# Pinning the projections that run beside a sliding-window attention, and moving its output bank through ScalarE

## The chip, the cores and the metric

The kernel runs on one core of a Trainium2 chip. The core has a matrix engine (TensorE, PE in the profile, with its weight loads on a row of their own, PEld), three engines for elementwise work (VectorE is DVE, ScalarE is ACT, GpSimd is POOL), a sync engine (SP) that here issues nearly all DMAs, an SBUF of 128 partitions and a PSUM of eight banks. The metric is the device time of one execution in microseconds; a comparison takes the median of several runs.

## The reference, cut to what matters

Two sequences (1024 and 512 tokens, width 1024) pass through two layers with shared weights. The change touches layer 0 only:

```python
u = rmsnorm(x, norm_g[0]) @ w_in0
glu, a_gate, q, k, v, b_gate = split_cols(u, EVEN_SPLITS)
a_val, a_glu = jnp.split(glu, 2, axis=-1)
a = layernorm(depthwise_conv(a_val * sigmoid(a_glu), conv_w, conv_b), ln_g, ln_b)
a = silu(a) * silu(a_gate)
o = windowed_gqa(rope(q), rope(k), v, sink) * silu(b_gate)     # +-128 tokens, 8 heads, 2 key heads
x = x + concatenate([a, o]) @ w_out0
```

Layer 1 (differential attention beside a two-way state-space scan) starts from the norm of this x and is not touched.

## The kernel before, in words

Tokens are cut into three chunks of 512: chunks 0 and 1 are the long sequence (the prompt), chunk 2 is the short one (the sample). Every projection works on tiles of 128 output channels by 512 tokens. All numbers are fp32, split into a rounded high part and a remainder, so one tile is 8 slices of the inner dimension by 3 products, that is 24 matmuls of 128x512 (`proj`, lines 294 to 296). The weights of a tile come in two halves: a DMA (L281), a cast on ScalarE (L282) and a subtraction on GpSimd (L283).

The stages around the change, in program order:

- Phase A1: the gated inputs of the convolution, k, v and q (with rotary), and meanwhile the depthwise convolution on VectorE (`conv_units`). Then `conv_ln` (L490): its first matmul (L494) takes the mean over channels from a sum that VectorE completes at L486. Then `ag(0)` and `ag(1)`: gate tiles, each with three chunks; `gate2` (L384) evacuates a tile with two ScalarE activations (L386, L387) into two buffers of the tag `e2`, one VectorE multiply (L388) and a DMA to DRAM. In A1 the tag has four shared buffers and two more (`e2x`); the weights have three shared and two more per kind (`wrx`, `whx`, `wlx`). Five PSUM banks serve the projections.
- Phase A2: the sliding attention. `swa_units(1)` (sample) gives a start and 8 units, `swa_units(0)` (prompt) a start and 16; a unit is one block of 128 queries with one key head. In a unit, `scores` issues eight matmuls (L568, L569) for four heads, VectorE adds the band and takes the maximum (L572), ScalarE exponentiates (L574) and GpSimd scales (L582); `values` of the unit before transposes the probabilities (L597), splits them (L215, L216) and accumulates two products per block of keys (L600, L601) in one PSUM bank `oacc` (tag `ms`, one bank). ScalarE copies one half of the partitions out (L602) and VectorE adds the other half from PSUM (L603). `spread` (L1027) hands groups of other units out between these units: gate tiles `ag`, `bg`, the loads of the concatenated input of an output projection (`so[g][1]`, `cat_units`, L622) and its eight output tiles (`so[g][2]`, `tile_` in `out_units`, L640).
- Phase B1a: the output tiles of chunk 0 and 1, the norms (`out_norm`), and the first projections of layer 1.

What sets the order on each engine: the program is not run in the order in which it is written. A scheduler at build time simulates the time line with its own instruction costs, and issues on each engine whatever its simulation finds ready, earlier code first. The order that comes out is fixed: on the chip each engine runs its list in order, and an instruction that waits holds up all behind it. `tc.issue_after(x)` adds a rule to that scheduler: the instructions in the block that run on the engine of x come behind x in its list. It adds no wait on the chip.

Buffers of a phase are placed in SBUF in the order of the dictionary in `PHASES` (L39), each phase over the ones before it; a buffer of a new phase can be filled when the old buffers under it are done with. With the sizes in the code (2 KB a partition for `e2`, `wr`, `wh`, `wl`, 4 KB for `cs`, `raw`, `q6` and `k4`, 6 KB for `y6`), `raw` of A2 lies over `e2x`, `wrx` and `whx` of A1, and `q6`, the last entry of A2, over the `y6` buffers that hold the convolution's result until it is written to `cat0d` (L509).

## Time and profile before

| | us |
|---|---|
| median of 3 runs (lowest, highest) | 1651.07 (1649.37, 1654.11) |
| the profiled execution, its own time | 1646.57 |
| its span, first to last instruction | 1644.8 |
| PE busy in the span | 1541.7 |
| VectorE busy | 1092.4 |
| ScalarE busy | 747.4 |
| GpSimd busy | 670.8 |
| mean granted TensorE clock | 0.987 |

Stretches are given in us from the start of the span. Busy time of PE counts a matmul from its start to a modelled end, so PE can be called busy while matmuls come slower than they could. A row of a time line gives start, duration, engine, line and operation, and in brackets how long the engine was idle before it and what ended that. The layer that is changed takes the first 700 us or so; the stretch from 299 to 660 holds all that the change touches.

### The profile page before, as it was taken

The page shows a single profiled execution, that of the slowest core. Times are in us where ns is not written, and L with a number is a line of the kernel's source. Part 1 is how long each engine was busy: PE and PEld are TensorE (multiplying, and loading weights), DVE is VectorE, ACT ScalarE, POOL GpSimd, SP SyncE. Part 2 cuts the span into 40 slices and gives each one's busy share as a digit, 9 for nine tenths or more (in the row PEclk, how much of TensorE's full clock was granted, in tenths as well). Part 3 has the DMA queues.
Part 4 walks back from the last instruction along what each step waited for, and adds up shares of the span by engine and source line. Part 5 has one row for each costly group of instructions (what it writes and reads, how often), then busy time and mean ns, then how long its engine had stood idle before and what let it go on. Part 6 is the DMA issues. An engine that isn't in the chain of part 4 may idle for free.

```text
span 1644.8 us, 22557 instructions
## 1 busy us (share of the span) xinstructions
PE 1541.7 (94%) x7772; PEld 1280.1 (78%) x7772; DVE 1092.4 (66%) x1568; ACT 747.4 (45%) x1461; POOL 670.8 (41%) x555
## 2 busy tenths in 40 slices
PE   4999899699989899999999999999989999999897
PEld 3888787478857777778788888878878888888787
DVE  6699999866688857565542005786537678678663
ACT  6312111266777754345442112222227777668532
POOL 4333543226766647432211006654435535341530
PEclk9999999899999999999999999999999999999999
DMA  9221123244556558613333217754454445342561
GB/s 371 70 68 42 45 84 92 94 159 143 162 172 192 167 165 264 203 58 91 112 126 116 77 45 218 212 173 152 133 172 139 142 152 167 116 133 73 182 232 67
DMA packets 159108, 229.43 MB, mean 139 GB/s; under 512 B 18279, under 2 KB 70567, under 8 KB 158994
## 3 DMA queue, kind: packets, MB, share of 16 engines
q1 hardware_dynamic: 157074, 227.40, 43.8%
q8 instruction: 61, 1.00, 0.3%
q0 software_dynamic: 1920, 0.59, 0.2%
q14 instruction: 53, 0.43, 0.1%
HBM read 153.15 MB, written 64.55 MB: 132 GB/s over the span
## 4 chain that ended last, share of the span: by engine, by line
PE 34%; DMA 5%; DVE 4%; issue 3%; ACT 2%; POOL 2%; SPq 1%; POOLq 0%; DVEq 0%; ACTq 0%
PE pj L294 4%; PE pj L295 4%; PE pj L296 4%; PE ms L994 3%; PE pjx L759 2%; PE pjx L760 2%; PE pjx L761 2%; PE s L978 2%; PE s L979 2%; PE pjx L296 2%; PE pjx L295 2%; PE pjx L294 2%; PE tr L406 1%; PE trx L406 1%; DMA ct<-g2d 1%
## 5 line engine op out<-in xcount | busy, mean ns | idle before, releaser
L283 POOL TENSOR_TENSOR wl<-wr,wh 128x512 fp32r<-128x512 f32 (+1 forms) x147 | 210.1, 1433 | 277.7 <-ACT wh L282 265.6
L295 PE MATMUL pjx<-x,wh 128*128 128x512 f32 (+1 forms) x576 | 227.6, 395 | 5.6 <-DVE x L216 5.6
L294 PE MATMUL pjx<-x,wh 128*128 128x512 f32 (+1 forms) x576 | 228.3, 397 | 3.0 <-DVE e L395 1.0
L296 PE MATMUL pjx<-x,wl 128*128 128x512 f32 (+1 forms) x576 | 227.7, 396 | 3.3 <-POOL wl L283 3.3
L294 PE MATMUL pj<-x,wh 128*128 128x512 f32 x536 | 215.8, 403 | 12.5 <-ACT e L387 4.4
L295 PE MATMUL pj<-x,wh 128*128 128x512 f32 x536 | 211.8, 395 | 4.5 <-DVE x L216 4.5
L296 PE MATMUL pj<-x,wl 128*128 128x512 f32 x536 | 213.1, 398 | 0.0
L282 ACT ACTIVATE wh<-wr 128x512 fp32r<-128x512 f32 (+1 forms) x147 | 91.5, 623 | 130.5 <-PE pjx L295 49.4
L295 PEld LDWEIGHTS pjx<-x,wh 128*128 128x128 f32 (+1 forms) x576 | 107.4, 186 | 30.8 <-DVE x L216 6.8
L294 PEld LDWEIGHTS pj<-x,wh 128*128 128x128 f32 x536 | 101.8, 190 | 37.1 <-ACT e L387 6.4
L294 PEld LDWEIGHTS pjx<-x,wh 128*128 128x128 f32 (+1 forms) x576 | 107.3, 186 | 29.3 <-ACT x L215 1.8
L296 PEld LDWEIGHTS pjx<-x,wl 128*128 128x128 f32 (+1 forms) x576 | 107.1, 186 | 28.0 <-POOL wl L283 4.1
L295 PEld LDWEIGHTS pj<-x,wh 128*128 128x128 f32 x536 | 101.7, 190 | 25.9 <-DVE x L216 6.0
L296 PEld LDWEIGHTS pj<-x,wl 128*128 128x128 f32 x536 | 101.7, 190 | 21.5 <-issue 0.5
L980 DVE TENSOR_REDUCE nmx<-s 128x1 f32<-128x1024 f32 (+1 forms) x96 | 97.9, 1040 | 23.5 <-PE s L979 23.0
L982 ACT ACTIVATE pr<-s,nmx 128x1024 f32<-128x1024 f32 (+1 forms) x96 | 93.4, 975 | 32.7 <-DVE nmx L980 29.1
L191 POOL TENSOR_TENSOR r<-v,mhalf 128x4 f32<-128x4 f32 (+2 forms) x37 | 33.4, 901 | 128.8 <-DVE v L187 76.5
L994 PEld LDWEIGHTS ms<-v,pT 128*128 128x128 f32 x640 | 78.5, 191 | 6.8 <-ACT m L996 2.0
L994 PE MATMUL ms<-v,pT 128*128 128x128 f32 x640 | 81.3, 276 | 2.2 <-ACT m L996 1.2
L532 POOL TENSOR_TENSOR raw<-raw,q 128x1024 fp32r<-128x1024 f32 x24 | 59.1, 2462 | 49.3 <-ACT q L530 38.7
L836 POOL TENSOR_TENSOR xd<-x,ed 128x512 f32<-128x512 f32 x20 | 23.2, 1161 | 125.5 <-DMA x<-xbd 120.6
L283 POOL TENSOR_TENSOR wlx<-wrx,whx 128x512 fp32r<-128x512 f32 x20 | 51.4, 2578 | 55.4 <-ACT whx L282 55.4
(415 smaller groups left out, 3786.9 us busy)
## 6 DMA issues: line engine op xcount, KB each, us to landing
wr<-in_wo SPq DMA_DIRECT2D x84, 256.0 KB, 4.2
wr<-in_w SPq DMA_DIRECT2D x71, 256.0 KB, 3.6
x<-xbd SPq DMA_DIRECT2D x22, 384.0 KB, 4.4
ct<-x1d SPq DMA_DIRECT2D x29, 256.0 KB, 4.3
raw<-q0d SPq DMA_DIRECT2D x48, 128.0 KB, 3.1
ct<-cat0d SPq DMA_DIRECT2D x24, 256.0 KB, 4.7
x1d<-e SPq DMA_DIRECT2D x24, 256.0 KB, 3.9
raw<-q1d SPq DMA_DIRECT2D x48, 128.0 KB, 2.8
```

The source lines that it names most:

```text
L191: G.tensor_tensor(out=r[:, 0:n], in0=v[:, 0:n], in1=mhalf[:, 0:n], op=ALU.pow)
L282: S.activation(out=wh, in_=raw, func=AF.Copy)
L283: G.tensor_tensor(out=wl, in0=raw, in1=wh.bitcast(F32), op=ALU.subtract)
L294: T_.matmul(acc, wh[:, kk, :], xh[:, k, :], start=(k == ks[0]), stop=False)
L295: T_.matmul(acc, wh[:, kk, :], xl[:, k, :], start=False, stop=False)
L296: T_.matmul(acc, wl[:, kk, :], xh[:, k, :], start=False, stop=(k == ks[-1]))
L406: T_.transpose(pt[:, t, :], src[:, t * P:(t + 1) * P], ident)
L532: G.tensor_tensor(out=lo, in0=raw, in1=q.bitcast(F32), op=ALU.subtract)
L759: T_.matmul(acc, xh[:, k, ts], hi[k], start=(k == 0), stop=False)
L980: V.tensor_reduce(out=nmx[:, t:t + 1], in_=o, axis=AX.XY, op=ALU.max, negate=True)
L982: S.activation(out=pr, in_=o, func=AF.Exp, bias=nmx[:, t:t + 1], accum_out=den[:, t:t + 1])
L994: T_.matmul(oacc, pT[:, i, :], vtok[:, kt, :], start=(kt == 0), stop=(kt == NB - 1))
```

## The change

The tail of A1 is written as `ag(0)`, `ag(1)`, `ag(2)`, then `conv_ln` with its mean matmuls behind the last matmul of `ag(2)`, then `ag(3)`. In A2 every handed-out unit's PE instructions go behind the first score matmul of the newest attention unit written so far (`ph["pin"]`), and the groups get other places: the chunk 2 gate tiles of `bg(2)` and `bg(3)` and then `bg(0)` and `bg(1)` over places 0 to 9, the sample's concatenated input over 9 to 14, the rest of `bg` over 9 to 13, the sample's eight output tiles over 13 to 23 with the statistics of its norm (`norm_r`) as a ninth unit, chunk 0's input over 18 to 22 and two of its output tiles over 23 to 25; the other six follow the attention. Before, `ag(2)`, `ag(3)` and eight `bg` tiles stood over 0 to 7, and the sample's output tiles over 21 to 26. `values` copies the whole bank `oacc` into a new buffer `both` by ScalarE and adds its two halves from there. In A2 the buffer list is reordered: `q6` follows `raw`, the sample's keys get two buffers of their own (`k2`), `k4` goes from 3 to 2, `pr` (probabilities) from 10 to 9.

```diff
--- before.py
+++ after.py
@@ -38,7 +38,7 @@
 
 PHASES = {
     "A1": (dict(e2x=2, wrx=2, whx=2, wlx=2, cs=2, a=2, xs=1, fir=3, y6=5), dict(pjx=4, msx=1)),
-    "A2": (dict(raw=3, v2=1, k4=3, v4=1, ct=3, ss=1, m2=1, sq=1, pT=5, pr=10, q6=2), dict(pjx=1, s1=3, trx=1)),
+    "A2": (dict(raw=3, q6=2, k2=2, v2=1, m2=1, pr=9, pT=5, k4=2, v4=1, ct=3, ss=1, sq=1, both=1), dict(pjx=1, s1=3, trx=1)),
     "B1a": (dict(ct=10, ss=1, sq=1, dt=3, m2=3, a=3, y6=2), dict(pjx=4, msx=1)),
     "B1z": (dict(zr=2, zw=8, vw=8), dict(pjx=5)),
     "B1b": (dict(e2x=1, wrx=1, whx=1, wlx=1, rk=2, lk=4, cs=2, p4=4, x3=2, bc=2, xd=2, y=2, t=1, nx=4, pb=1, yc=2, zt=1), dict(sg=1, msx=2, trx=1)),
@@ -293,7 +293,7 @@
             with nullcontext() if after is None or k < k0 else tc.issue_after(after.ins):
                 T_.matmul(acc, wh[:, kk, :], xh[:, k, :], start=(k == ks[0]), stop=False)
                 T_.matmul(acc, wh[:, kk, :], xl[:, k, :], start=False, stop=False)
-                T_.matmul(acc, wl[:, kk, :], xh[:, k, :], start=False, stop=(k == ks[-1]))
+                ph["proj"] = T_.matmul(acc, wl[:, kk, :], xh[:, k, :], start=False, stop=(k == ks[-1]))
         return acc
 
     phase("A1")
@@ -487,11 +487,12 @@
 
         return [begin] + [lambda i=i: taps(i, i + 3) for i in range(1, 16, 3)] + [end]
 
-    def conv_ln():
+    def conv_ln(pin):
         sm = cvs["s"]
         for g in GO:
             mu = pm("ms")
-            T_.matmul(mu, mean_w, sm[:, g, :], start=True, stop=True)
+            with tc.issue_after(pin.ins):
+                T_.matmul(mu, mean_w, sm[:, g, :], start=True, stop=True)
             for j in range(4):
                 y = cv[j][:, g, :]
                 V.tensor_tensor(out=y, in0=y, in1=mu, op=ALU.subtract)
@@ -515,7 +516,7 @@
             raw = sb("raw", (P, T))
             for a in range(2):
                 dma(out=raw[64 * a:64 * a + 64], in_=src[64 * t:64 * t + 64, t0:t0 + T])
-            kt = sb("k4", (P, T), F32R)
+            kt = sb("k2" if T == CH and "k2" in ph["sb"] else "k4", (P, T), F32R)
             S.activation(out=kt, in_=raw, func=AF.Copy)
             G.tensor_tensor(out=kt[lr], in0=raw[lr], in1=kt[lr].bitcast(F32), op=ALU.subtract)
             kk.append(kt)
@@ -565,8 +566,10 @@
             prs = st_[b, g] = []
             for j in range(4):
                 o = pm("s1")[:, 0:nk * P]
-                T_.matmul(o, qh[:, g, j, :], kk[g][:, k0 * P:k1 * P], start=True, stop=False)
+                first = T_.matmul(o, qh[:, g, j, :], kk[g][:, k0 * P:k1 * P], start=True, stop=False)
                 T_.matmul(o, ql[:, g, j, :], kk[g][:, k0 * P:k1 * P], start=False, stop=True)
+                if j == 0:
+                    ph["pin"] = first
                 mx = nmx[:, j:j + 1]
                 pr = sb("pr", (P, 384))[:, 0:nk * P]
                 V.tensor_tensor_reduce(out=pr, in0=o, in1=band[:, (0 if k0 < b else P):(3 * P if k1 > b + 1 else 2 * P)], scale=-1.0,
@@ -599,8 +602,9 @@
                 split_into(pt, ph_, pl_, V)
                 T_.matmul(oacc, vtok[:, k0 + kb, g, :], ph_, start=(kb == 0), stop=False)
                 T_.matmul(oacc, vtok[:, k0 + kb, g, :], pl_, start=False, stop=(kb == nk - 1))
-            S.activation(out=ot[hr], in_=oacc[hr], func=AF.Copy)
-            V.tensor_tensor(out=ot[hr], in0=ot[hr], in1=oacc[64 - 64 * g:128 - 64 * g], op=ALU.add)
+            both = sb("both", QUAD)
+            S.activation(out=both, in_=oacc, func=AF.Copy)
+            V.tensor_tensor(out=ot[hr], in0=both[hr], in1=both[64 - 64 * g:128 - 64 * g], op=ALU.add)
             if g:
                 dma(out=catd[0][:, 4:8, t0 + b * P:t0 + (b + 1) * P], in_=ot)
 
@@ -656,8 +660,13 @@
 
         return st_, load(st_), [lambda j=j: tile_(j) for j in range(KT)]
 
+    def norm_r(st_):
+        st_["r"] = rstd_of(tok_sum([st_["ss"]]), 4, 1.0 / DM)
+
     def out_norm(st_, spill, g, gcol, last):
-        bc = tok_bcast(rstd_of(tok_sum([st_["ss"]]), 4, 1.0 / DM), 4, False)
+        if "r" not in st_:
+            norm_r(st_)
+        bc = tok_bcast(st_["r"], 4, False)
         if not last:
             xh, xl = x16(), x16()
         for k in range(KT):
@@ -1024,15 +1033,15 @@
         for u in f[j:]:
             u()
 
-    def spread(a, groups):
+    def spread(a, groups, pin=False):
         at = [[] for _ in range(len(a) + 1)]
         for f, p0, p1 in groups:
             for i, u in enumerate(f):
                 at[min(len(a), p0 + i * (p1 - p0) // len(f))].append(u)
         for i, u in enumerate(a):
-            run(at[i])
+            run(at[i], pin)
             u()
-        run(at[-1])
+        run(at[-1], pin)
 
     def tile_units(i, w, fn, order=(2, 0, 1)):
         st_ = {}
@@ -1060,9 +1069,10 @@
     def bg(j, order=N3):
         return tile_units(14 + j, w0, lambda acc, g: gate2(acc, gd[1][:, j, tok(g)]), order)
 
-    def run(us):
+    def run(us, pin=False):
         for u in us:
-            u()
+            with tc.issue_after(ph["pin"].ins) if pin and "pin" in ph else nullcontext():
+                u()
 
     gl = [glu_units(j) for j in range(4)]
     cu = [conv_units(j, gl[j][0]) for j in range(4)]
@@ -1073,23 +1083,27 @@
     merge(gl[2][1] + q[1], cu[1])
     merge(gl[3][1] + q[2], cu[2])
     merge(q[3] + q[4] + q[5], cu[3])
-    conv_ln()
-    run(ag(0) + ag(1))
+    run(ag(0) + ag(1) + ag(2))
+    conv_ln(ph["proj"])
+    run(ag(3))
 
     phase("A2")
     res0 = lambda g, j: xin(g)[:, j, :]
     so = [out_units(wo0, lambda st_, g=g: cat_units(st_, catd[0], {k: gd[k // 4] for k in range(8)}, g), res0, x1d, g, 4) for g in range(3)]
     uS, uP = swa_units(1), swa_units(0)
     spread(uS + uP, [
-        (ag(2) + ag(3) + bg(0) + bg(1) + bg(2, (2,)) + bg(3, (2,)), 0, 7),
-        (so[2][1], 11, 19),
-        (bg(2, (0, 1)) + bg(3, (0, 1)), 9, 17),
-        (so[0][1], 19, 19),
-        (so[2][2], 21, 26)])
+        (bg(2, (2,)) + bg(3, (2,)) + bg(0) + bg(1), 0, 9),
+        (so[2][1], 9, 14),
+        (bg(2, (0, 1)) + bg(3, (0, 1)), 9, 13),
+        (so[2][2] + [lambda: norm_r(so[2][0])], 13, 23),
+        (so[0][1], 18, 22),
+        (so[0][2][:2], 23, 25)], True)
+    run(so[0][2][2:4])
     out_norm(so[2][0], x1d, 2, PC_G1, False)
+    run(so[0][2][4:])
+    norm_r(so[0][0])
 
     phase("B1a")
-    run(so[0][2])
     run(so[1][1])
     out_norm(so[0][0], x1d, 0, PC_G1, False)
     run(so[1][2])
```

## Rows read from the trace of the kernel before

**Rows 1.** Busy time of each engine in eight stretches (columns: stretch, its length, PE, PEld, DVE, ACT, POOL with the number of instructions, granted TensorE clock, DMA share, GB/s).

```profile
299.00:324.00 25.00, 11.93 (x42) 8.72 (x41) 23.95 (x28) 5.09 (x9) 1.58 (x1) 0.73 0.23 79
324.00:378.00 54.00, 52.95 (x252) 43.30 (x252) 30.89 (x41) 31.74 (x51) 17.85 (x12) 1.00 0.55 180
378.00:461.00 83.00, 82.91 (x428) 69.85 (x427) 54.74 (x127) 60.40 (x147) 59.15 (x64) 1.00 0.49 149
461.00:500.00 39.00, 30.45 (x142) 21.36 (x140) 33.12 (x82) 29.05 (x78) 22.75 (x30) 0.96 0.53 155
500.00:555.00 55.00, 53.88 (x275) 45.36 (x274) 42.36 (x87) 39.09 (x91) 39.40 (x43) 1.00 0.61 187
555.00:589.00 34.00, 25.85 (x133) 19.11 (x131) 30.18 (x78) 25.95 (x69) 18.29 (x28) 0.95 0.57 181
589.00:610.00 21.00, 21.00 (x101) 17.30 (x100) 9.38 (x26) 9.42 (x20) 9.72 (x11) 1.00 0.45 133
610.00:660.00 50.00, 46.14 (x210) 37.56 (x209) 34.05 (x42) 21.94 (x39) 32.50 (x23) 0.97 0.80 252
```

**Rows 2.** The same stretches for L294 alone, the first of the three matmuls of a projection's slice (columns: stretch, length, PE, PEld with counts, clock, DMA share, GB/s); eight of them are one tile.

```profile
299.00:324.00 25.00, 5.44 (x13) 2.72 (x13) 0.73 0.23 79
324.00:378.00 54.00, 26.16 (x67) 12.43 (x67) 1.00 0.55 180
378.00:461.00 83.00, 32.17 (x82) 15.24 (x81) 1.00 0.49 149
461.00:500.00 39.00, 2.56 (x7) 1.24 (x8) 0.96 0.53 155
500.00:555.00 55.00, 19.73 (x49) 9.06 (x49) 1.00 0.61 187
555.00:589.00 34.00, 0.00 (x0) 0.01 (x1) 0.95 0.57 181
589.00:610.00 21.00, 10.47 (x26) 4.88 (x26) 1.00 0.45 133
```

**Rows 3.** The same for L568 alone, the first matmul of a head's scores; four of them are one attention unit.

```profile
378.00:461.00 83.00, 11.05 (x37) 6.76 (x37) 1.00 0.49 149
461.00:500.00 39.00, 8.07 (x21) 3.96 (x21) 0.96 0.53 155
500.00:555.00 55.00, 6.64 (x19) 3.58 (x19) 1.00 0.61 187
555.00:589.00 34.00, 7.38 (x19) 3.85 (x19) 0.95 0.57 181
```

**Rows 4.** Time line of PE from 304.9 to 324 us, cut.

```profile
304.57 0.39 PE L295 MATMUL pjx<-x,wh 128*128 128x512 f32 x1
304.80 0.39 PE L296 MATMUL pjx<-x,wl 128*128 128x512 f32 x1
...
305.93 0.39 PE L295 MATMUL pj<-x,wh 128*128 128x512 f32 x1
319.39 2.07 PE L494 MATMUL msx<-y,mean_w 128*128 128x512 f32 x2 [13.07 <-DVE y L486]
...
322.12 0.63 PE L295 MATMUL pj<-x,wh 128*128 128x512 f32 x1
322.54 0.63 PE L296 MATMUL pj<-x,wl 128*128 128x512 f32 x1
```

**Rows 5.** Time line of VectorE from 312 to 324 us: the last step of the sum that L494 reads.

```profile
317.58 1.76 DVE L486 TENSOR_TENSOR y<-y,y 128x1536 f32<-128x1536 f32 x1
```

**Rows 6.** Time line of ScalarE from 307 to 382 us, cut to the casts of the first keys and queries and the table load before the first exponential.

```profile
325.44 0.63 ACT L519 ACTIVATE k<-raw 128x512 fp32r<-128x512 f32 x1 [13.31 <-DMA raw<-k0d]
...
372.36 2.01 ACT L530 ACTIVATE q<-raw 128x1024 fp32r<-128x1024 f32 x2 [2.67 <-DMA cat0d<-y]
...
381.25 1.28 ACT L574 ACT_TABLE_LOAD   x1
```

**Rows 7.** Time line of SP's DMA issues from 319 to 367 us, cut.

```profile
319.96 0.32 SPq L389 DMA_DIRECT2D g0d<-e2x  x1
322.01 2.41 SPq L517 DMA_DIRECT2D raw<-k0d  x4
...
327.53 8.48 SPq L553 DMA_DIRECT2D raw<-q0d  x12
...
362.64 3.06 SPq L509 DMA_DIRECT2D cat0d<-y  x3
```

**Rows 8.** Time line of GpSimd from 320 to 382 us, cut: the subtractions of the first keys and of the first two queries.

```profile
326.20 2.66 POOL L520 TENSOR_TENSOR k<-raw,k 64x512 fp32r<-64x512 f32 x2 [15.60 <-ACT k L519]
...
373.50 5.22 POOL L532 TENSOR_TENSOR raw<-raw,q 128x1024 fp32r<-128x1024 f32 x2 [7.98 <-ACT q L530]
```

**Rows 9.** Time line of PE from 377.5 to 381 us: the first score matmuls.

```profile
378.09 0.52 PE L568 MATMUL s<-k,q 128*128 128x256 f32 x3
```

**Rows 10.** Two VectorE additions by line, over the sliding attention (columns: duration in ns as least, median and most; first and last start; form). The first has one input in PSUM, the second two in SBUF.

```profile
L603 DVE TENSOR_TENSOR m<-m,ms x24: 682/687/691, 403.0 to 610.0; 64x512 f32<-64x512 f32 x24
L655 DVE TENSOR_TENSOR ss<-ss,sq x9: 686/811/2885, 506.7 to 610.9; 128x512 f32<-128x512 f32 x9
```

**Rows 11.** Who waited for whom from 290 to 660 us (total us, times, longest), PE and VectorE, cut.

```profile
PE pjx L296 <- POOL wl L283: 3.3, 2, 2.8
...
PE ms L600 <- DVE m L603: 2.6, 3, 1.2
...
DVE pr L572 <- POOL pr L582: 2.3, 2, 1.2
DVE pr L572 <- PE trx L597: 2.0, 3, 0.8
```

## The prediction, made before the changed kernel was run

> **What bounds the kernel now.** PE is busy for 94% of the span, so only time in which it stands still or is slowed can be won. I cut the stretch that the change touches into eight and read engine times, then the count of projection matmuls (a tile is eight of L294) and of score matmuls (a unit is four of L568) [rows 1 to 3]. Three stretches stand out.
>
> First, 299 to 324: PE is busy for 11.9 of 25 us while VectorE is busy for 23.9 [rows 1]. The time line shows why. At 305.9 PE has begun the first tile of `ag(2)`, five matmuls in, and the next in its list is the mean matmul L494, which waits 13.07 us for L486, the end of the convolution on VectorE [rows 4, 5]. The projections behind it need nothing from it. The granted clock of the stretch is 0.73, and after the idle time matmuls start 0.42 us apart where they started 0.23 apart before [rows 4]: half of 2.4 GHz, until about 324.
>
> Second, the attention. In 378 to 461 and 500 to 555 PE is busy throughout (136.8 of 138 us). These hold 82 + 49 of L294, 16.4 tiles, and 37 + 19 of L568, 14 units. A tile takes 24 x 0.227 = 5.45 us [rows 4], so the tiles take 89 us and a unit (136.8 - 89) / 14 = 3.4 us of PE [rows 1 to 3]. In 461 to 500 and 555 to 589 there are only 7 of L294 and 40 of L568: 5 + 34 = 39 us of PE work in 73 us. So 34 us are lost where the units have no projections beside them; there VectorE is at 85% and 89% and paces them at 7.3 us a unit. In the two full stretches it is at 66% and 77%. The work is there, in the wrong place.
>
> Third, the first score comes only at 378.1 [rows 9]. The keys were cast at 325 and the query loads issued from 327.5, but the query cast waited until 372.4 for a write to `cat0d` [rows 6, 7]: `q6` lies over the convolution's result. By then ten tiles had been used up (80 of L294 from 299 to 378 [rows 2]) that the units lack later.
>
> **The change, part by part, against the profiled execution (1646.6).**
>
> *Front.* The matmuls of `ag(2)` no longer wait behind L494, and three tiles end at about 305.9 + 2.8 x 5.45 = 321, when the sum (319.3) is ready. The 13 us wait and the slow clock behind it (six and more matmuls with 0.2 us each and the slow L494 itself, some 2 to 3 us) go. What is late next is the first score. `q6` now lies over `wlx` and `cs`, free once the last `ag` tile has run, and `raw` still over `e2x`, `wrx`, `whx`, which `ag(3)` now uses. From 305.9 PE has 2.8 + 3 tiles of `ag`, so `ag(3)` ends near 338. Then the chain follows: key loads (2.4 us of issue), cast, subtraction 2.7, query loads (a third of 8.5), cast 1.0, subtraction 2.6 [rows 6 to 8], with some 3 us of landing each, about 18 us: the first score can come at 356 to 361. PE has for that time the two `bg` tiles that no pin holds and the small matmuls of `conv_ln` (about 8 us): 299 + 9.1 x 5.45 + 8 = 357. I take 361, for a few us of gap: 17 us won, between 4 (the evacuation of `ag(2)` stalls on `e2` buffers while VectorE still works off the convolution) and 21.
>
> The moved tiles take their queues with them: each of `ag(2)` and `ag(3)` issues two weight loads on SP (0.3 to 0.4 us each), two casts on ScalarE and two subtractions on GpSimd, now ahead of the key loads. At 305.9 the weights of `ag(2)` were there, and those of `ag(3)` have 15 us, so nothing for that. `conv_ln` is put off by some 2 us on PE; VectorE and ScalarE are its only waiters, and its result in `cat0d` is first read at place 9, tens of us later: nothing.
>
> *Loop.* The units must hold 12 `bg` tiles less 2, 8 + 2 output tiles: 20 tiles, where 20.5 ran before [rows 2]. PE needs 20 x 5.45 + 24 x 3.4 = 191 us of the 232 now spent. VectorE's 169.8 us (five stretches of rows 1) become some 178 with the dearer additions below; at the 0.87 it reaches where it sets the pace, 205 us. That is the floor. The ceiling is 228, the old length less half a tile: gates and concatenated loads crowd places 9 to 13 and 18 to 22, where VectorE has more than a unit's time to do. The pins keep a tile from being used before the unit ahead has begun, so the starved stretches should go, the crowded ones not. I take 216, the middle: 16 us won.
>
> *What is owed.* Fewer tiles are done by the end of the attention: 10 + 20.5 before, 9.1 + 20 after, 1.4 x 5.45 = 7.5 us to be paid there.
>
> *The copied bank.* ScalarE's copy costs the same: 128 or 64 partitions by 512 columns. `oacc` is released after the copy instead of after L603; PE waited 2.6 us in all for that [rows 11]. The addition takes two SBUF inputs. L603 never took over 0.69 us; L655, with two SBUF inputs, took 0.69 to 2.9, median 0.81 [rows 10], and GpSimd is busy for some 149 of these 232 us [rows 1]. So 24 additions cost 24 x 0.12 = 3 to 24 x 0.5 = 12 us of VectorE; I took 8 in the loop. The Trainium skill, SBUF — State Buffer, section SBUF: two separate sides, speaks against this edit: VectorE with two SBUF inputs and GpSimd exclude one another for a whole instruction. The spread of L655 beside the fixed L603 agrees; by the rule alone I would take the upper bound, 12 us instead of 8, and the loop's floor would be 209.
>
> *Smaller.* `pr` 10 to 9: VectorE waited 4.3 us for such buffers [rows 11]; one fewer may double that, 0 to 4 us, I take 1. Separate key buffers: no wait for them is seen, nothing. Exponentials may now fall between the SiLUs of `conv_ln`; each turn costs a table load of 1.28 us [rows 6] on ScalarE, which is busy 59% of the time then; 0 to 5, I take 0.5. The waits on weights at 630 to 640 (3.3 us [rows 11]) stay. `norm_r` early: its one short chain now lies beside units, nothing.
>
> Sum: -17 - 16 + 7.5 + 1.5 = -24, so 1622.6 profiled. The median lies 4.5 us above the profiled execution: 1627.
>
> **The rivals.**
>
> *Better.* Front 21 and loop 205: -21 - 27 + 7.5 = -40, 1611. For it: PE full for 138 us wherever projections stand beside units. Against: VectorE would have to hold 87% throughout.
>
> *VectorE paces the loop anyway.* The loop stays at 228: -17 - 4 + 9 = -12, 1639. For it: 85 and 89% in the starved stretches, and added work; against: 66 and 77% in the full ones.
>
> *The pinned mean changes little.* `ag(2)` is stuck behind the evacuation, VectorE being busy at 95% until 324 [rows 1]: front 4, loop 16: 1646.6 - 4 - 16 + 9 = 1636, 1640 by the median. Against: there are five banks, and PE had begun the first tile of `ag(2)` when it stopped.
>
> *Slower: whole tiles in the chain.* A pin fixes only the earliest place. If the scheduler, whose costs are not the chip's, places a tile's 24 matmuls in one piece between the first score and the rest of that unit, the unit's chain of score, maximum, exponential, transposes and products waits 5.45 us more: 7.3 + 5.45 = 12.7 us a unit, against 9 in the forecast, so each tile so placed costs 3.7 us. With 16 of 20 it costs 59: 1646.6 - 24 + 59 = 1682, 1686; with 10 it costs 37, 1664. It decides from 24 / 3.7 = 7 tiles on. Against: before, the tiles in the full stretches are cut into pieces between scores (the first score itself stands between two projection matmuls).
>
> *It does not do what it says.* The planner in its own time line had no starved stretch, and the tiles keep their places: what the front runs ahead is missing between the units later, and it stays at 1647 to 1655.
>
> **How the numbers follow.** Forecast (1617 to 1634) 0.46; better 0.13; VectorE paces 0.13; the mean changes little 0.08; no change 0.08; slower 0.12. A measurement of this kernel can tell 0.3%, 5 us, from no change. Faster, below 1646: 0.46 + 0.13 + 0.13 + 0.08 = 0.80. Same 0.08. Slower 0.12. The range runs from 1600, past the better case by its uncertain front, to 1653, which takes in no change and leaves out the slower case: about 0.17 outside.
>
> **What would show each step.** Front: L494 without a wait of over 3 us, no stretch near 0.73 clock before 330, the first L568 at 356 to 365, L530 not released by `cat0d`. Loop: from first score to last transpose 205 to 228 us, L294 in every 40 us of it, VectorE at 80% or more. Addition: L603's successor above 0.69 us with a spread. The slower case would show as PE waits on L572 or L216 right behind unbroken runs of 24 projection matmuls. If the first score comes no earlier than 370, my reading of the buffers is wrong.

## The result, and the profile after

The changed kernel takes 1638.77 us (median of 5 runs, 1635.6 to 1639.6) where the kernel before took 1649.37 beside it: a ratio of 0.994, 95% interval 0.992 to 0.9959. That is 10.6 us faster, where 24 were forecast. The profiled execution took 1638.8 us (span 1636.8, granted clock 0.982), 7.8 less than the one of before.

Engine time in stretches, as in [rows 1], with bounds where the changed kernel has its own:

```profile
299.00:324.00 25.00, 24.94 (x109) 20.01 (x108) 24.93 (x25) 6.70 (x12) 6.84 (x4) 1.00 0.17 64
324.00:357.00 33.00, 33.00 (x163) 27.36 (x162) 23.42 (x40) 23.65 (x40) 13.06 (x10) 1.00 0.46 148
357.00:400.00 43.00, 40.47 (x204) 33.58 (x203) 23.88 (x59) 33.30 (x73) 26.11 (x27) 1.00 0.63 206
400.00:440.00 40.00, 31.68 (x142) 25.43 (x143) 26.21 (x52) 23.79 (x56) 27.04 (x28) 0.87 0.48 131
440.00:540.00 100.00, 95.36 (x487) 78.24 (x485) 74.70 (x171) 71.24 (x174) 69.02 (x75) 1.00 0.59 180
540.00:560.00 20.00, 16.49 (x78) 12.94 (x77) 16.60 (x39) 15.19 (x38) 14.10 (x16) 0.91 0.52 165
560.00:620.00 60.00, 59.93 (x309) 50.07 (x308) 42.52 (x83) 34.44 (x81) 35.97 (x41) 1.00 0.60 193
620.00:640.00 20.00, 15.75 (x54) 11.38 (x53) 18.02 (x34) 10.81 (x19) 10.43 (x7) 0.74 0.91 312
```

The front is as forecast: full, at full clock. The starved stretches of before, 461 to 500 and 555 to 589, are much fuller. But there are holes in other places, at 400 to 440, at 540 to 560 and behind the attention, and in them the mean granted clock falls to 0.87, 0.91 and 0.74. Projections, by L294 as in [rows 2] (the last row is the whole attention):

```profile
299.00:324.00 25.00, 14.02 (x36) 6.57 (x35) 1.00 0.17 64
324.00:357.00 33.00, 15.54 (x40) 7.34 (x39) 1.00 0.46 148
400.00:440.00 40.00, 8.99 (x22) 4.43 (x22) 0.87 0.48 131
357.00:621.00 264.00, 83.08 (x209) 39.45 (x208) 0.97 0.58 178
```

26 tiles run inside the attention, not the 20 that I counted: the scheduler drew all eight output tiles of chunk 0 in between the last units, though six are written behind them. Two rows of PE's time line answer to [rows 4, 9], the mean matmul, now without a wait, and the first score:

```profile
323.03 1.12 PE L495 MATMUL msx<-y,mean_w 128*128 128x512 f32 x2
...
357.51 0.52 PE L569 MATMUL s<-k,q 128*128 128x256 f32 x3
```

What PE waited for from 357 to 621 us (total us, times, longest), the main rows:

```profile
PE ms L604 <- DVE pT L216: 5.0, 4, 2.9
PE s L569 <- DVE nmx L575: 4.1, 3, 2.6
PE ms L603 <- ACT both L606: 3.7, 2, 3.1
PE trx L600 <- DVE pT L216: 2.3, 1, 2.3
```

**One measure for all kernels.** Every kernel below but those that say so does the same matmuls. I count each at about the spacing at which it follows another without a wait (0.225 us for 512 columns, 0.12 for 256, 0.065 for 128; a tile is 5.4 us). The sum up to a moment is the PE work done; the time beyond it is called lost: to waits, to the half clock and to small gaps between matmuls. The count is too low for the transposes of the attention: in before, the changed kernel, `b_order` and `a_best` one follows another at 0.108 to 0.109 us (the median) where I count 0.065. That puts 8 to 9 us into each "lost" of these four that no filler could save; it is nearly the same in all, so the differences stand. For the attention, first score to last value product (worked out from the traces, us):

```
kernel          first score  last product  length  work in it   lost
before             378.1        609.0       230.9     184.5     46.4
changed            357.5        620.3       262.7     215.7     47.0
a_nopin            360.7        614.2       253.6     211.9     41.7
b_order            377.6        598.7       221.0     168.5     52.6
b_front            381.0        600.5       219.5     165.8     53.7
a_keys             358.4        622.6       264.3     212.5     51.7
a_early            357.8        617.5       259.6     213.9     45.7
a_tail             357.1        594.6       237.5     184.1     53.4
a_nolo             358.6        604.0       245.5     208.5     37.0
b_nolo             376.6        597.9       221.3     182.4     38.9
b_frontnolo        379.8        591.4       211.6     165.5     46.0
a_best             358.1        614.6       256.5     213.7     42.8
```

And the lead over before at equal PE work (negative: ahead of before; at 250 the profile of before is 0.9 to 2.8 us quicker than these):

```
work    before    changed  b_order  b_front  a_nopin   a_cat   a_best
 250     290.0      +2.1     +0.9     +2.8     +2.6     +2.0     +1.0
 275     336.7     -17.3    -18.5    -16.1    -16.2    -17.5    -18.8
 375     442.9      +2.1    -18.2    -13.8     -6.4     +1.7     -8.3
 425     513.2      -8.5    -11.5     -5.7    -11.8    -10.5    -13.9
 525     642.8     -22.5    -11.0     -8.5    -26.8    -23.4    -28.2
 550     668.7     -13.1    -11.0     -6.6    -17.5    -14.8    -22.1
 850     981.4     -12.9    -11.1     -7.5    -17.0    -14.5    -21.8
1375    1627.4      -8.8     -8.2     -7.4    -14.5    -7.0    -21.6
```

The changed kernel wins 19 us at the front, loses all of it by 443 us, is 17 us ahead again by 520 of work, where before was starved, gives up 4 of them behind the attention, and 4 more from 850 on, in code that the change does not touch. The 22.5 at 525 is no gain of its own: there before stands in its own hole, waiting 3.3 us for weights [rows 11] with a clock of 0.95 from 620 to 640, and the changed kernel's hole comes a little later. From 620 to 640 us before loses 6.2 us and the changed kernel 9.4.

### The profile page after: what moved, and what is told of

Same layout as the page of the kernel before. It is cut to its first block, busy times and chain, and to the rows that moved or that the text cites. A ratio compares the mean times of both kernels' runs of the same rounds, so it can differ in the third digit from the quotient of the medians.

```text
span 1636.8 us, 22539 instructions
## 1 busy us (share of the span) xinstructions
PE 1547.2 (95%) x7772; PEld 1286.9 (79%) x7772; DVE 1081.9 (66%) x1568; ACT 749.2 (46%) x1463; POOL 677.8 (41%) x555
## 4 chain that ended last, share of the span: by engine, by line
PE 36%; DMA 5%; DVE 4%; issue 3%; ACT 2%; POOL 1%; SPq 1%; POOLq 0%; DVEq 0%; ACTq 0%
PE pj L294 4%; PE pj L295 4%; PE pj L296 4%; PE ms L1003 3%; PE pjx L770 2%; PE pjx L769 2%; PE pjx L768 2%; PE s L987 2%; PE s L988 1%; DMA ct<-g2d 1%; PE pjx L296 1%; PE pjx L295 1%; PE pjx L294 1%; PE tr L406 1%; PE trx L406 1%
## 5 line engine op out<-in xcount | busy, mean ns | idle before, releaser
L294 PE MATMUL pj<-x,wh 128*128 128x512 f32 (+1 forms) x540 | 219.1, 406 | 11.9 <-ACT e L387 6.6
L295 PE MATMUL pjx<-x,wh 128*128 128x512 f32 (+1 forms) x548 | 217.7, 398 | 5.4 <-DVE x L216 4.7
L294 PE MATMUL pjx<-x,wh 128*128 128x512 f32 (+1 forms) x548 | 217.8, 399 | 4.5 <-ACT x L215 4.5
L295 PE MATMUL pj<-x,wh 128*128 128x512 f32 (+1 forms) x540 | 216.3, 400 | 4.8 <-DVE x L216 4.8
L296 PE MATMUL pjx<-x,wl 128*128 128x512 f32 (+1 forms) x548 | 217.1, 397 | 0.0
L296 PE MATMUL pj<-x,wl 128*128 128x512 f32 (+1 forms) x540 | 215.2, 399 | 1.0 <-POOL wl L283 1.0
L294 PEld LDWEIGHTS pj<-x,wh 128*128 128x128 f32 (+1 forms) x540 | 102.9, 191 | 36.6 <-ACT e L387 9.4
L295 PEld LDWEIGHTS pjx<-x,wh 128*128 128x128 f32 (+1 forms) x548 | 103.5, 189 | 29.7 <-DVE x L216 6.3
L295 PEld LDWEIGHTS pj<-x,wh 128*128 128x128 f32 (+1 forms) x540 | 102.9, 190 | 28.0 <-DVE x L216 7.3
L294 PEld LDWEIGHTS pjx<-x,wh 128*128 128x128 f32 (+1 forms) x548 | 103.5, 189 | 27.0 <-ACT x L215 4.9
L296 PEld LDWEIGHTS pj<-x,wl 128*128 128x128 f32 (+1 forms) x540 | 102.7, 190 | 23.3 <-POOL wl L283 1.3
L296 PEld LDWEIGHTS pjx<-x,wl 128*128 128x128 f32 (+1 forms) x548 | 103.2, 188 | 22.4
L989 DVE TENSOR_REDUCE nmx<-s 128x1 f32<-128x1024 f32 (+1 forms) x96 | 97.7, 1039 | 20.8 <-PE s L988 20.5
L585 POOL TENSOR_SCALAR pr<-pr,den 128x384 f32<-128x384 f32 (+1 forms) x96 | 62.5, 668 | 28.6 <-DVE den L583 15.0
L738 DVE SCALAR_TENSOR_TENSOR y<-a,prm,y 128x1536 f32<-128x1536 f32 x32 | 59.1, 1848 | 21.9 <-ACT y L735 21.4
```

The source lines that it names most:

```text
L294: T_.matmul(acc, wh[:, kk, :], xh[:, k, :], start=(k == ks[0]), stop=False)
L295: T_.matmul(acc, wh[:, kk, :], xl[:, k, :], start=False, stop=False)
L296: ph["proj"] = T_.matmul(acc, wl[:, kk, :], xh[:, k, :], start=False, stop=(k == ks[-1]))
L585: G.tensor_scalar(out=prs[j], in0=prs[j], scalar1=den[:, j:j + 1], scalar2=1.0, op0=ALU.mult, op1=ALU.mult)
L738: V.scalar_tensor_tensor(out=acc, in0=a[:, :, t:t + CH], scalar=prm[:, wc + t:wc + t + 1], in1=acc, op0=ALU.mult, op1=ALU.add)
L989: V.tensor_reduce(out=nmx[:, t:t + 1], in_=o, axis=AX.XY, op=ALU.max, negate=True)
```

## The experiments

Ratios are to the kernel before, run beside each (5 rounds), with their 95% interval.

**The front alone.** `b_front` is before with these lines and the new buffer order (old sizes); `b_order` the same with the old buffer order.

```diff
-    conv_ln()
-    run(ag(0) + ag(1))
+    run(ag(0) + ag(1) + ag(2))
+    conv_ln(ph["proj"])
+    run(ag(3))
...
-        (ag(2) + ag(3) + bg(0) + bg(1) + bg(2, (2,)) + bg(3, (2,)), 0, 7),
+        (bg(0) + bg(1) + bg(2, (2,)) + bg(3, (2,)), 0, 7),
```

> The kernel before with the front of the change alone: three tiles of gates ahead of the normalisation, its sums held behind them, and the new order of the buffers. The spread of the rest, the keys' buffers and the half copy stay as before. If the front's gain (16 to 20 us of PE time at the first score, measured in the changed kernel) survives on its own: 1627 to 1631, and the rest of the change is then worth nothing or less. If the attention gives it back, because the first units stand without gates beside them: 1640 or above. If the changed spread is what earns: some 1636 to 1640, between.

> The kernel before with the front's order alone (three tiles of gates ahead of the normalisation, its sums held behind them), the attention's buffers laid out as before. If the order alone makes the front's gain: no wait above 3 us and no half clock between 300 and 330, and PE 16 us ahead at 336 as with both. If the first query and key loads still wait for the normalised tiles' buffers: the gain at 336 is there, but the first units lose it, and PE is 8 us or less ahead by 364.

`b_front`: 1638.35 us, 0.9949 (0.9931 to 0.9967). `b_order`: 1638.32, 0.9947 (0.9926 to 0.9969). Each alone gains as much as the whole change. The order does it; the buffers do not. Here is `b_order` from 299 to 324, then ScalarE's first query cast in it and in `b_front`:

```profile
299.00:324.00 25.00, 24.98 (x109) 20.05 (x108) 24.48 (x25) 6.70 (x12) 5.61 (x3) 1.00 0.21 75
```

```profile
373.47 2.01 ACT L531 ACTIVATE q<-raw 128x1024 fp32r<-128x1024 f32 x2 [4.02 <-DMA wr<-in_w]
```

```profile
357.55 1.06 ACT L531 ACTIVATE q<-raw 128x1024 fp32r<-128x1024 f32 x1 [0.44 <-POOL r L191]
```

So the layout was read rightly, it frees the first query 16 us sooner, but nothing comes of it here: PE is full from 324 to 378 anyway, and in `b_front` the first score is at 381. What counts is the idle time that goes, 19 us at 275 of work. The attention then takes back 11 us of it between 375 and 400 of work, of which `b_order` wins 4 back later: the 16 to 17 us of work that PE does ahead of the first score are missing there. Its work falls by 16.0 us in `b_order` and 18.7 in `b_front`, its length by 9.9 and 11.4.

**The pins.** `a_nopin` is the changed kernel with `(so[0][2][:2], 23, 25)])` instead of `..., True)`.

> The changed kernel with the same spread of projections and output tiles, but none of them held behind the unit after which it is due. If the pins do the work (projections stay where PE waits for the softmax chain): 5 to 15 us above the changed kernel's 1638.8, with waits back in the loop. If the pins hold PE back: below it. If the list scheduler places them much the same by itself: within 4 us.

1632.04 us (1630.0 to 1632.5), 0.9903 (0.9884 to 0.9922): faster than with pins, against the theory that they do the work (the two intervals just touch). Between `b_front` and `a_nopin` lie the new places, the key buffers and the copied bank together, 0.0046; the places alone were not run. The loss in the attention falls from 47 to 42 us. In the stretch below it falls by 9.7, and from 460 to 500 us 4.4 of that are lost again:

```profile
400.00:440.00 40.00, 37.54 (x190) 30.26 (x189) 26.47 (x53) 26.05 (x61) 25.73 (x26) 1.00 0.44 133
```

**The hole at 400 to 440.** In the changed kernel ScalarE stands three times, from 393 to 412 us, at the casts of the prompt's keys and values, and on SP the second key load is issued 10 us behind the first, behind a gate's store (L389) that itself waits for ScalarE and VectorE:

```profile
394.93 1.06 ACT L520 ACTIVATE k<-raw 128x1024 fp32r<-128x1024 f32 x1 [2.00 <-DMA raw<-k0d]
404.11 1.06 ACT L520 ACTIVATE k<-raw 128x1024 fp32r<-128x1024 f32 x1 [5.01 <-DMA raw<-k0d]
411.95 1.06 ACT L547 ACTIVATE v<-raw 128x1024 fp32r<-128x1024 f32 x1 [2.96 <-DMA raw<-v0d]
```

```profile
389.58 1.11 SPq L518 DMA_DIRECT2D raw<-k0d  x2
399.07 0.33 SPq L389 DMA_DIRECT2D g1d<-e  x1
399.56 0.44 SPq L518 DMA_DIRECT2D raw<-k0d  x1
```

That was my first theory of the missing gain. `a_keys` holds these casts on ScalarE behind the newest exponential of the sink term (kept as `ph["pina"]`):

```diff
         def start():
+            with tc.issue_after(ph["pina"].ins) if "pina" in ph else nullcontext():
+                start_()
```

`a_early` writes the prompt's key and value loads (`uP[0]`, without its first query load) behind the sample's second unit, `a_nopinearly` does so without pins:

```diff
+    early, uS2, uP = uP[0], uS[2], uP[1:]
+    uS[2] = lambda: (uS2(), early())
```

`a_gq` issues the store in `gate2` from GpSimd:

```diff
-        dma(out=dst, in_=t)
+        nc.gpsimd.dma_start(out=dst, in_=t)
```

> The changed kernel, with the prompt's first key and value casts and its first query cast held on ScalarE until the last sample unit's tiny exponential is done. Queue theory (in-order ScalarE casts of late keys and values stop PE at 404 to 430 us, 13 us of PE time lost there in the changed kernel): 395 to 430 us loses under 4 us and the time is 8 to 12 us below the changed kernel's, about 1628. VectorE theory (the loop is paced by VectorE, with dearer additions from two SBUF tiles): what is saved at 395 to 430 is lost again before the last value product, the time is within 3 us of the changed kernel's. Third case: the casts come too late for the prompt's first unit, PE waits some 5 us at the sample's end, within 3 us or slower.

> The changed kernel with the loads and casts of the prompt's keys and values issued seven units earlier (beside the sample's second unit; the first query load stays where it was). Queue theory for the stretch from 395 to 430 us (ScalarE stands at the cast of a late key, the gate's store waits for ScalarE's and VectorE's results, and the next key load stands behind that store on SyncE): no wait of ScalarE above 1 us for a key load after 385, PE loses 6 instead of 16 us from 400 to 440, time 4 to 8 us below the changed kernel's 1638.8. If those holes are VectorE's, or are only moved: within 3 us.

> The same early loads in the changed kernel without its pins (1632 measured). Queue theory: what is left of that loss without pins is 3 to 4 us, so 1627 to 1630. If unpinned fillers cover it already: 1630 to 1635.

> The changed kernel with the gates' stores of the first stage issued by GpSimd instead of SyncE, so that no key load stands behind one. Queue theory: the second key load is issued within 2 us of the first one (10 us apart in the changed kernel), and 3 to 6 us are gained, unless GpSimd's own list, which now waits for VectorE's gates, costs as much. Otherwise within 3 us.

`a_keys`: 1643.12, 0.9976 (0.9959 to 0.9993), nearest to its third case: it loses 18 us from 400 to 460. `a_early`: 1637.82, 0.9945 (0.9926 to 0.9964). `a_nopinearly`: 1634.58, 0.9921 (0.9892 to 0.995). `a_gq`: 1644.87, 0.9995 (0.9977 to 1.0012). None gains on its base. `a_early` does what it should: no wait for a key load is left, and 400 to 440 is better filled. Yet the time is the same, for the holes stand elsewhere:

```profile
380.00:400.00 20.00, 16.07 (x73) 12.91 (x72) 15.06 (x19) 13.13 (x30) 17.26 (x13) 0.91 0.64 199
400.00:440.00 40.00, 36.91 (x190) 31.03 (x189) 28.59 (x68) 28.16 (x70) 22.77 (x30) 0.96 0.37 112
460.00:480.00 20.00, 14.27 (x62) 12.04 (x60) 12.09 (x29) 10.41 (x26) 10.07 (x14) 0.83 0.65 202
```

So the late keys explain where that hole is, not how much is lost in all, and as the cause of the missing gain the theory falls. In `a_nopin` the second key is cast as late, at 405.8 us, and 400 to 440 loses 6.2 us where the changed kernel loses 15.9. That fits pins that keep fillers out of this hole; no run tests it alone.

**The copied bank.** `a_noboth` is the changed kernel with the old two lines behind the products, `a_nopinnoboth` the same without pins, `b_both` before with the new ones (and `pr` at 9 instead of 10, to make room). The first two:

```diff
-            both = sb("both", QUAD)
-            S.activation(out=both, in_=oacc, func=AF.Copy)
-            V.tensor_tensor(out=ot[hr], in0=both[hr], in1=both[64 - 64 * g:128 - 64 * g], op=ALU.add)
+            S.activation(out=ot[hr], in_=oacc[hr], func=AF.Copy)
+            V.tensor_tensor(out=ot[hr], in0=ot[hr], in1=oacc[64 - 64 * g:128 - 64 * g], op=ALU.add)
```

> The changed kernel with the old output step: half of the bank copied by ScalarE, the other half added from PSUM by VectorE; all else stays. Queue theory: the additions cost VectorE some 0.2 us more each but lie off the path, time within 4 us of the changed kernel's 1638.8. VectorE theory (24 additions, some 0.36 us dearer each by their mean of 864 against 687 ns plus the wait for the longer copy): 5 us or more below it.

> The kernel before with the copied bank alone: the whole bank copied by ScalarE, the halves added from SBUF, one buffer less for the scores. Dearer additions on the path (24 of them, some 0.2 to 0.4 us dearer each): 4 to 9 us above before. Off the path: within 3 us of before, as its removal from the changed kernel moved less than 2 us.

> The changed kernel without pins and with the old half copy. VectorE theory: the 24 additions are some 11 us longer in all with the copied bank (1168 against 687 ns); without it 3 to 5 us below the 1632 of the kernel without pins. If the bank that comes free earlier is worth as much: 1630 to 1636.

`a_noboth`: 1640.54, 0.9965 (0.9949 to 0.998). `b_both`: 1651.85, 1.0026 (1.001 to 1.0043). `a_nopinnoboth`: 1633.38, 0.9927 (0.9907 to 0.9947). On before the copy with one `pr` buffer less costs 4 us; no run tells the two apart. In the changed kernel, with `pr` at 9 in both, the times lie 4 us better with the copy, with and without pins, but the intervals overlap. It is no large part of the gap.

**VectorE.** In the `nolo` kernels (`a_nolo` of the changed kernel, `b_nolo` of before, `b_frontnolo` of `b_front`) the low half of the transposed scores is left out (the second product takes the high half again): 64 subtractions less, PE's work the same.

```diff
-                split_into(pt, ph_, pl_, V)
+                S.activation(out=ph_, in_=pt, func=AF.Copy)
...
-                T_.matmul(oacc, vtok[:, k0 + kb, g, :], pl_, start=False, stop=(kb == nk - 1))
+                T_.matmul(oacc, vtok[:, k0 + kb, g, :], ph_, start=False, stop=(kb == nk - 1))
```

> The changed kernel without the low halves of the transposed scores (the subtraction that makes them is left out, and the second value product takes the high half again), so that VectorE has some 68 operations of 0.68 us less in the sliding attention, 46 us, while PE's work is the same. VectorE theory (PE's 47 us lost in the attention are VectorE's bursts ahead of scores and values): the loss falls to 25 us or less and the time by 15 us or more, to about 1622. Queue theory (in-order lists and late loads): the time falls by less than 8 us.

> The kernel before without the low halves of the transposed scores (the subtraction is left out, the second value product takes the high half again): 26 to 46 us less of VectorE's work in the attention, PE's work the same. It is the base for the next run. VectorE theory: before's attention is paced by the same chain, 8 to 16 us below before. If the loss before is of late data and order: under 4 us below.

> The same, with the front of the change alone. With the low halves the front's 18.9 us at its end were down to 7.4 by the kernel's end. VectorE theory (the front took fillers that had stood beside units paced by VectorE, and the units without them idle): with VectorE relieved, more of the front's gain is kept, 12 to 18 us below the run without the front. If the front's gain is lost to order and late data whatever VectorE does: 5 to 9 us below it.

`a_nolo`: 1623.06, 0.9869 (0.9842 to 0.9896). `b_nolo`: 1639.86, 0.9965 (0.9947 to 0.9984). `b_frontnolo`: 1630.97, 0.9908 (0.9884 to 0.9931). From first score to last value product VectorE has 38 us less to do, first the changed kernel, then `a_nolo`:

```profile
357.50:620.30 262.80, 243.73 (x1213) 200.09 (x1212) 183.91 (x401) 177.47 (x420) 171.73 (x184) 0.97 0.58 179
```

```profile
358.60:604.00 245.40, 232.34 (x1180) 193.51 (x1179) 146.07 (x335) 174.75 (x417) 165.06 (x181) 0.98 0.60 186
```

The loss in the attention falls by 10 us, and by 7.5 and 7.7 in the other two. For `a_nolo` and `b_nolo` that is between the two theories, so what was taken out has a share, but most of the loss stays when a fifth of VectorE's work is gone. The edit does more than unload VectorE: the second value product no longer waits for the subtraction, and a buffer of `pT` is saved. The runs do not tell these apart. The pair `b_nolo` and `b_frontnolo` decides the other question: the front is worth 0.0057 (9 us) with VectorE relieved, 0.0051 (8 us) without. VectorE's load is not why the front's gain is lost.

**Behind the last product.** In the changed kernel PE waits there for the first input of chunk 1's output tiles. VectorE is 18 of 20 us busy, and two of its splits take 1.76 us where the third takes 0.68. The two start while GpSimd has a split of its own running, the third when GpSimd is done (PE, then VectorE one by one, then GpSimd):

```profile
625.74 1.22 PE L294 MATMUL pjx<-x,wh 128*128 128x512 f32 x2 [2.91 <-ACT x L215]
```

```profile
626.33 1.76 DVE L216 TENSOR_TENSOR x<-ct,x 128x512 fp32r<-128x512 f32 x1
628.01 1.76 DVE L216 TENSOR_TENSOR x<-ct,x 128x512 fp32r<-128x512 f32 x1
629.70 0.68 DVE L216 TENSOR_TENSOR x<-ct,x 128x512 fp32r<-128x512 f32 x1
```

```profile
625.82 3.41 POOL L216 TENSOR_TENSOR x<-ct,x 128x512 fp32r<-128x512 f32 x2
```

`a_tail2` and `a_tail` hold the last two or six output tiles of chunk 0 behind the last product, `a_nopintail` is `a_tail` without pins in the attention. This is `a_tail` (`ph["end"]` is the newest value product; `a_tail2` holds only `[6:]`):

```diff
-    run(so[0][2][2:4])
+    ph["pin"] = ph["end"]
+    run(so[0][2][2:4], True)
     out_norm(so[2][0], x1d, 2, PC_G1, False)
-    run(so[0][2][4:])
+    run(so[0][2][4:], True)
```

`a_cat`, and `a_best` without pins, form four of the eight inputs earlier instead:

```diff
+    run(so[1][1][:4])
     run(so[0][2][2:4])
...
-    run(so[1][1])
+    run(so[1][1][4:])
```

> The changed kernel with only the last two of the first stage's eight output tiles held behind the last value product. Queue theory (nothing is left beside the chain from the last attention output to the next stage's input; 9 us of PE time lost in 620 to 640 us at half clock): the two tiles of about 3.3 us each fill it, no wait above 2 us there, time 5 to 8 us below the changed kernel's, about 1632. VectorE theory: the same tiles were needed as filler between units, the attention ends as late as they are moved, time within 2 us.

> The changed kernel with six of the first stage's eight output tiles held behind the last value product (two were not enough: their additions stood behind 5.7 us of splits on VectorE). If the chain from the last attention output to the next stage only needs enough tiles beside it, as before the change: the 9 us lost there fall to 3 or less, and what the units between 590 and 620 us lose without those tiles is less than that; 3 to 6 us below the changed kernel. If the same tiles are needed between the units just as much: within 3 us of it or above.

> The changed kernel without the pins in the attention (1632 measured) and with six output tiles held behind the last value product. If both losses are separate, the late units' fillers and the tail: 3 to 6 us below 1632. If the tiles only move the loss from the tail into the attention: 1630 to 1636.

> The changed kernel with the first four inputs of the next stage's second output group (those from the convolution and its gate, which need no attention output) formed ahead of the last attention units instead of behind them. If the 9.4 us given back behind the last value product are the chain of multiplications and splits for eight inputs on VectorE and ScalarE: half of the chain stands earlier, PE starts the next tiles without a wait above 1.5 us and without half clock at 620 to 640, time 4 to 7 us below the changed kernel's 1638.8. If only the last attention output's way through DRAM counts: within 2 us, since its four inputs come as late as before. If VectorE in the last units is full: the loss moves there, within 2 us.

> The same early inputs in the changed kernel without pins (1632 measured). Chain theory: 4 to 7 us below it, 1625 to 1628, the fastest of all with the whole computation. Otherwise 1630 to 1634.

`a_tail2`: 1644.81, 0.9988 (0.9972 to 1.0004). `a_tail`: 1646.85, 1.0 (0.9983 to 1.0018). `a_nopintail`: 1645.12, 1.0002 (0.9983 to 1.002). Held tiles cost 8 to 16 us: the last units have less beside them (the attention of `a_tail` loses 53 us), and PE waits for additions of those tiles (L648), 8.4 us in `a_tail2`, where they are queued on VectorE behind 5.7 us of splits, and 5.5 us in the other two. `a_cat`: 1640.05, 0.9959 (0.9943 to 0.9975), no gain. `a_best`: 1627.48 (1625.0 to 1630.7), 0.9883 (0.9866 to 0.99), the fastest with the whole computation: 19 us below before, its interval clear of the changed kernel's (it still touches that of `a_nopin`). From 620 to 640, `a_cat` and `a_best`:

```profile
620.00:640.00 20.00, 16.91 (x70) 13.16 (x69) 15.37 (x21) 8.73 (x14) 8.00 (x6) 0.91 0.91 314
```

```profile
620.00:640.00 20.00, 16.78 (x68) 11.66 (x67) 16.50 (x20) 8.69 (x15) 8.96 (x7) 1.00 0.98 351
```

From 520 of work, ahead of the hole of before, to 550 the changed kernel gives up 3.7 us of its lead, `a_cat` 3.0, `a_nopin` 3.4 and `a_best` 0.3. So without pins the early inputs take this loss away (by one trace of each kernel); with pins they move almost nothing, and why stays open.

## Why the prediction was right and wrong, step by step

**Front, -17: right.** The first score came 20.6 us earlier, within 4 to 21; L495 has no wait, the clock is full, 9.5 tiles stand before the first score (9.1 forecast), and the query cast no longer waits for `cat0d`. But two causes were counted as one. `b_order` shows that the moved tiles alone bring the gain; the buffer layout works as I read it and, on before, is worth nothing measurable. The changed kernel with the old layout was not run.

**Loop, -16: the step that failed.** I wrote that the pins keep fillers for the starved stretches, "so the starved stretches should go", and took 39 us of loss (232 less 20.5 tiles and 24 units) down to 25. By the same count it stayed at 40: the loop took 262.7 us with 25.9 tiles in it, where I had 216 with 20. The old holes did shrink: 460 to 500 lost 18.2 us before and 8.7 after, 560 to 600 lost 15.1 and 3.5. But 400 to 440 now loses 15.9 (2.8 before) and 540 to 560 7.4 (4.0), and the sum is what it was, 46.4 and 47.0. The error was to treat the loss as a lack of fillers. It moved little when they were taken out, added, pinned or freed: 16 to 19 us of work out raised it by 6 to 7 (`b_order`, `b_front`); 27 us in lowered it by 5 without pins, 31 us in with pins by nothing. So in these kernels a microsecond of filler saved 0.2 to 0.4 without pins, and nothing with them, where I reckoned with most of it. PE runs its list in order, and all that the profile has it wait for from 357 to 621 us is 17 us in before ([rows 11] hold one part, L600 on L603) and 19 in the changed kernel. Worked out with the same spacings, another 4 and 6 us are lost while the clock is down, 9 and 8 to the pace of the transposes, and the rest, 17 and 14, to small gaps. So about half of the loss is no wait that a filler could cover. What puts the waits where they are in each order was not settled. The pins themselves cost 4 to 12 us: the unpinned partner is faster by 0.0037 (plain), 0.0024 (early loads), 0.0038 (half copy) and 0.0076 (early inputs). The intervals of the last two pairs are apart, those of the first touch, those of the second overlap. Only with held tiles are the two the same.

VectorE was not the floor either: 0.70 of the attention, where I took 0.87 as the limit. Taking 38 us of its work away brought 10.

**What is owed, +7.5: wrong in its premise.** I let six tiles follow the attention, as written. They were drawn in, 26 tiles instead of 20. The attention is 31.8 us longer with 26.4 us more PE work done by its end, so loop and debt together are +5.4 where I had -8.5. Behind it nothing covers the inputs of chunk 1 any more: the waits on weights there, which I left standing, went, and 4.1 us of waits for inputs took their place.

**The sum for the profiled executions**: -20.6 at the first score, +5.4 in the attention, +2.3 from there to 850 of work, +4.9 after that: -8.0 in the span. The last two parts I had at nothing. `b_front` has none of the last, the kernels built on the changed one have 0 to 8. On the way, at 1100 of work, the changed kernel is level with before and then wins 9 back; I have not found the cause.

**Copied bank and smaller things, +1.5: about right as a time.** The addition, as in [rows 10]:

```profile
L607 DVE TENSOR_TENSOR m<-both x24: 684/864/2581, 389.2 to 621.6; 64x512 f32<-64x512 f32 x24
```

That is above 0.69 with a spread, as written, and in the attention 23 of them take 26.9 us, 0.48 us more each, the upper end of my 3 to 12 us. The trace shows why. All 14 additions over 0.69 us start while a GpSimd instruction runs, and each ends 0.53 to 0.55 us behind that one; of the other 10, nine start with none running and one with 0.1 us of it left. The longest, VectorE then GpSimd:

```profile
422.79 2.58 DVE L607 TENSOR_TENSOR m<-both 64x512 f32<-64x512 f32 x1
```

```profile
422.46 2.36 POOL L533 TENSOR_TENSOR raw<-raw,q 128x1024 fp32r<-128x1024 f32 x1 [1.30 <-ACT q L531]
```

The Trainium skill (SBUF — State Buffer, section SBUF: two separate sides) says that a VectorE instruction with two SBUF inputs and a GpSimd instruction that reads SBUF exclude one another for the whole instruction. These rows agree with it.

So the price of the edit depends on what GpSimd does just then. The addition shown holds up the maximum behind it on VectorE, and PE waits 2.6 us for that, until 426.3. But on the whole VectorE had the room, and `a_noboth` without these additions is no faster. One `pr` buffer less raised VectorE's waits for such buffers from 4.3 us to 11.0, where I thought of a doubling; no run changes that count alone. Separate key buffers, which I put at nothing, go with prompt loads that are early enough to stop ScalarE (not tested by themselves); `a_early` shows that this is not what the kernel lacks.

**The rivals.** The number of "VectorE paces the loop anyway" (1639) came out, not its mechanism: VectorE at 0.70, and the loop is longer, not 228. "It does not do what it says" had the right thought, that what the front runs ahead is missing between the units, but as a no-change case; `b_order` and `b_front` show that it takes about half of the front's gain. Of the slower case nothing is seen: no wait in the attention is above 3.1 us.

## What to carry to other kernels

A hole filled with work that stood in another hole's neighbourhood is won once and lost in part: ask first what the moved work was covering (here 19 us won, 8 to 9 left at the end). Stretches in which PE waits are not filled in proportion to the work put beside them, least of all by rules that fix where it may start; count the loss over the whole loop, at equal work, before and after, not the stretches that went, and see first how much of it is waits. And a unit written behind a loop may run inside it: read its place from the trace before costing it as owed.

## What was not expected of the hardware

Short holes were paid about twice in the changed kernel. From 400 to 440, around waits of 2.6 and 3.1 us, PE stood still for 8.3 us, the granted clock was 0.87 and 15.9 us were lost; from 620 to 640, around waits of 2.9, 0.6 and 0.6, it stood still for 4.3, the clock was 0.74 and 9.4 were lost. In `a_best` PE stood still for 3.2 us from 620 to 640, the clock stayed at 1.00 and 5.2 were lost.

A VectorE instruction with two inputs in SBUF counts as busy while it is held up by GpSimd: an addition that takes 0.69 us alone took up to 2.58. So VectorE's busy share is in part waiting, and PE waited 0.6 us for a split held up like this.
